# Sums of squares on VectorE, and a low half of weights placed behind the inputs

## The chip, the cores and the metric

One core of one Trainium2 chip. The metric is the device time of one execution in microseconds (us), lower is better. TensorE is called PE, VectorE DVE, ScalarE ACT and GpSimd POOL; SP issues the weight DMAs. L12 is line 12 of the kernel.

## The reference

Two blocks of two layers each work on 256 tokens of width 1024, in float32, one behind the other. Every layer is x = x + mixer(rms_norm(x)), then x = x + mlp(rms_norm(x)); the mixers are a convolution with a gated recurrence (HGRN), stick-breaking attention, a state-space model (S5) with a gated linear unit (GLU), and forgetting attention (fox). The first block modulates its norms and gates with vectors that come from c @ ada_w.

```python
def rms_norm(x, g):
    xf = x.astype(jnp.float32)
    y = xf * lax.rsqrt(jnp.mean(xf * xf, axis=-1, keepdims=True) + EPS)
    return (y * g.astype(jnp.float32)).astype(x.dtype)

def sqrelu_mlp(h, w1, w2):
    a = jnp.square(jax.nn.relu(h @ w1))
    return a @ w2

# one layer of the first block
h = rms_norm(x, norm_mix[layer]) * (1.0 + scale1) + shift1
x = x + gate1 * mixer(h)
h = rms_norm(x, norm_mlp[layer]) * (1.0 + scale2) + shift2
x = x + gate2 * (jnp.square(jax.nn.relu(h @ mlp_w1[layer])) @ mlp_w2[layer])
```

What matters here is the mean of x*x over the 1024 features, of which every norm needs one, and that every product is made to float32's precision.

## The kernel before

The state x lies transposed in SBUF as xT: eight tiles of 128 features by 256 tokens. Every float32 product is made from two halves in the fast format fp32r. ACT copies a weight tile `raw` (128x2048, 1 MB) into its high half `wh`, and DVE makes the low half `wl` = raw - wh; the same is done with the inputs, of which X holds the high halves XH and the low halves XL. A product is wh*XH + wh*XL + wl*XH. Plain 128x128 weights by 256 columns are one matmul.

Weights come as a stream of such tiles, called units, in the order of a plan. `pump` issues a unit's DMA from SP as soon as one of six raw tiles is free; `unit_ahead` makes the halves of up to two units more than the one in use (three pairs of wh and wl tiles), and `release` frees the raw tile once the low half is made. A tuple DMALO names units whose low half would be made by an accumulating DMA; it is empty.

The stages run one after the other: layer 0's mixer (l0), its MLP (mlp0), stick breaking (sb), the second MLP (mlp1), s5 with glu, the third MLP (mlp2), fox, the fourth MLP (mlp3). At the end of each the last products of a stage are finished in eight pieces m = 0 to 7 by three functions: `fin` adds the piece to xT on DVE; `a` makes the next stage's XH of that piece on ACT (`prep_h`) and its square (`square`); `b`, called one piece later, makes XL on DVE (`prep_l`). `square` lets ACT write x*x into one of two tiles sqt, or into sqa for piece 0, and lets POOL add it to sqa. `stats` then multiplies sqa by a matrix of 1/1024 on PE, which adds over the partitions, and ACT turns the result into the scales that the norm needs. At two places (`last=NK - 2`) only five of the seven adds are made, and stats takes the last two squares by themselves. The norm's scale is applied behind the first products, so those start before stats is done.

Order: on POOL and SP it is the program's. On the other engines a list scheduler orders the instructions by priority and by its own costs, except for DVE in s5 with glu and ACT in mlp2 and mlp3, where it is the program's too (ORDER). `behind(later, first, why)` tells the scheduler that one instruction stands behind another on the same engine; no semaphore comes of it. Modulation vectors are made by dot products on DVE (L688, `ada_next`) which are spread over the stages at low priority.

Of the kernel before, what the change touches and what calls it, by code (L numbers as in the profile page):

```python
# [10 lines left out]
F32 = mybir.dt.float32  # L11
F32R = mybir.dt.float32r  # L12
U8 = mybir.dt.uint8
AF = mybir.ActivationFunctionType
# [6 lines left out]
ADD, SUB, MUL, MAX, MIN = ALU.add, ALU.subtract, ALU.mult, ALU.max, ALU.min  # L21

T = 256
D = 1024
NK = D // 128
# [13 lines left out]

DMALO = ()
S5SEQ = "g P0 P1 g T0 T1 TB0 M0 P2 P3 TB1 Q0 Q1 T2 T3 g Q2 Q3"


# [197 lines left out]
class Later:  # L244


    def __init__(self, prog):
        self.ops = []
        for n in ("tt", "ts", "stt", "act", "table", "copy"):
            setattr(self, n, partial(self.do, getattr(prog, n)))  # L250
# [23 lines left out]
class Prog:  # L274
    def __init__(self, ctx, tc, a, out):
        self.ctx, self.tc, self.nc, self.a, self.out = ctx, tc, tc.nc, a, out
        self.vcost = 0.0
        self.bank_last = {}
        self.set_load, self.set_uses = None, []
        self.const = ctx.enter_context(tc.tile_pool(name="const", bufs=1))  # L280
        self.psum = ctx.enter_context(tc.tile_pool(name="ps", bufs=1, space=bass.MemoryType.PSUM))
        self.pball = self.psum.tile([128, 8, 512], F32, name="psall")
        self.pb = [self.pball[:, i, :] for i in range(8)]
# [113 lines left out]
    def unit_ahead(self, ahead, between=None):  # L397

        last = min(self.used_n + ahead, len(self.wseq) - 1)
        while self.split_n <= last:  # L400
            j = self.wseq[self.split_n]
            if j not in self.slot:
                assert self.split_n > self.used_n, ("not loaded", self.plan[j][1])
                break
            b = self.split_n % len(self.hb)
            raw = self.raw_of(j)
            if self.plan[j][1] in DMALO:
                self.act(self.hb[b], raw, AF.Copy)
                self.release(j)
                lo = self.lb[b]  # L410
                self.act(lo, self.hb[b].bitcast(F32), AF.Copy, scale=-1.0)
                self.nc.gpsimd.dma_start(out=lo, in_=self.a["wst"][self.wpos[j]], accum_op=ADD)
                self.split_n += 1
                continue
            n = 1 + (self.plan[j][1][0] in HALVES)
            parts = [slice(i * 2048 // n, (i + 1) * 2048 // n) for i in range(n)]
            for c in parts:
                self.act(self.hb[b][:, c], raw[:, c], AF.Copy)
            if between is not None:
                between()  # L420
                between = None
            for c in parts:
                self.tt(self.lb[b][:, c], raw[:, c], self.hb[b][:, c].bitcast(F32), SUB)
            self.release(j)
            self.split_n += 1
        if between is not None:
            between()
# [76 lines left out]
                wh, wl = (t[:, k, m * 128:(m + 1) * 128] for t in (hv, lv))  # L504
                self.pair(outs[m], wh, wl, self.X2[S][:, k], k == 0, k == NK - 1)

    def rows_mm(self, units, xs, banks, start, stop, evac=None, late=False):

        kt = [(h, l, j) for h, l in units for j in range(2)]
        out = lambda m: self.pb[banks[m // 2]][:, (m % 2) * T:(m % 2 + 1) * T]  # L510
        if evac is not None:
            fin, a, b = evac
        if late:
            for q, m in [(q, m) for q in range(2) for m in range(NK)]:
                h, l, j = kt[q]
                w = h[:, j * D + m * 128:j * D + (m + 1) * 128]
                self.mm(out(m), w, xs[q][0], q == 0 and start and m % 2 == 0, False)
                self.mm(out(m), w, xs[q][1], False, False)
            for q, m in [(q, m) for q in range(2) for m in range(NK)]:
                h, l, j = kt[q]  # L520
                self.mm(out(m), l[:, j * D + m * 128:j * D + (m + 1) * 128], xs[q][0], False, q == 1 and stop and m % 2 == 1)
            return
        for m in range(NK):
            o = out(m)
            for q, (h, l, j) in enumerate(kt):
                c = j * D + m * 128
                xh, xl = xs[q]
                wh, wl = h[:, c:c + 128], l[:, c:c + 128]
                self.mm(o, wh, xh, q == 0 and start and m % 2 == 0, False)
                self.mm(o, wh, xl, False, False)  # L530
                self.mm(o, wl, xh, False, q == len(kt) - 1 and stop and m % 2 == 1)
            if evac is not None and m % 2 == 1:
                for i in (m - 1, m):
                    fin(i, out(i))
                    a(i)
                    if i:
                        b(i - 1)
        if evac is not None:
            b(NK - 1)
# [11 lines left out]
        self.act(self.XH[S][:, m, :T], self.xT[:, m, :], AF.Copy, scale=A[:, m:m + 1])  # L551

    def prep_l(self, S, m, A):
        self.stt(self.XL[S][:, m, :], self.xT[:, m, :], A[:, m:m + 1], self.XH[S][:, m, :T].bitcast(F32), MUL, SUB)

    def prep_shift(self, S, B):
        h = self.XH[S][:, :, 256:257]
# [3 lines left out]
    def square(self, i, last=NK):  # L561

        s = self.sqt[i % 2] if i else self.sqa
        self.act(s, self.xT[:, i, :], AF.Square)
        if 0 < i < last:
            self.nc.gpsimd.tensor_tensor(out=self.sqa, in0=self.sqa, in1=s, op=ADD)  # L566

    def stats(self, bank, std=False, rstd=False, r2=False, epv=False, tok=False, parts=None):
        ps = self.pb[bank]
# [382 lines left out]
    def mlp(self, tag, S, finish, side=(), after=None, before=None):  # L952
        n = DFF // 256
        with self.tc.tile_pool(name="pm" + tag, bufs=1) as p:
            hh = [p.tile([128, 2, T], F32R, name=f"hh{i}") for i in range(3)]
            hl = [p.tile([128, 2, T], F32R, name=f"hl{i}") for i in range(3)]
            tt_ = [p.tile([128, 2, T], F32, name=f"ht{i}") for i in range(2)]
            wb = [p.tile([128, 2], F32, name=f"wb{i}") for i in range(2)]
            yb = (0, 1, 2, 3)

            def A(u):
                b = 4 + 2 * (u % 2)
                t = s = tt_[u % 2]
                ps = [self.pb[b], self.pb[b + 1]]
                self.proj_T((tag + "a", u), S, ps, n=258, parts=1 + (u == 0))
                if u == 0:
                    self.stats(6, std=True, r2=True)
                w = wb[u % 2]
                self.red(w, self.pball[:, b:b + 2, 256:258], ADD)
                for m in range(2):  # L970
                    self.stt(t[:, m, :], self.stdb, w[:, m:m + 1], ps[m][:, :T], MUL, ADD)
                self.act(t, t, AF.Relu)
                self.act(s, t, AF.Square)
                self.act(hh[u % 3], s, AF.Copy)
                self.tt(hl[u % 3], s, hh[u % 3].bitcast(F32), SUB)

            def B(us, fin=None):
                ws = [self.unit((tag + "b", u), ahead=2 - i) for i, u in enumerate(us)]
                xs = [(hh[u % 3][:, j, :], hl[u % 3][:, j, :]) for u in us for j in range(2)]
                self.rows_mm(ws, xs, yb, us[0] == 0, us[-1] == n - 1, fin, (tag + "b", us[0]) in DMALO)  # L980

            def sides(b):
                self.side_banks = (b, b + 1)
                for g, budget in side:
                    start = self.vcost
                    while next(g, "end") == "more" and self.vcost - start < budget:
                        pass

            A(0)
            for u in range(1, n - 1):  # L990
                A(u)
                sides(6 - 2 * (u % 2))
                if u == n - 2:
                    A(n - 1)
                B([u - 1])
                sides(4 + 2 * (u % 2))
            for g, _ in side:
                for _ in g:
                    pass
            if after is not None:  # L1000
                after()
            if before is not None:
                before()
            B([n - 2, n - 1], finish)

    def mlp_finish(self, gate, nxt):
# [824 lines left out]
```

## Time and profile before

| | us |
|---|---|
| median of three runs | 1313.73 |
| lowest and highest | 1310.88, 1315.62 |
| the profiled execution | 1311.48 |
| its span, first to last instruction | 1309.7 |

The profile is of one execution. Busy time is that of an engine's own instructions; a wait is the idle time of an engine before an instruction, put down to what released it last. A name such as `X<-xTt,mod,X` is what an instruction writes and reads; buffer numbers are left out. Consecutive DVE instructions overlap in the rows: one can begin a little before the row of the one before it has ended, so the distance of two starts is less than a row's length.

### The profile page before, as it was taken

What the parts mean: (1) busy time and instruction counts of PE and PEld (TensorE: products, weight loads), DVE (VectorE), ACT (ScalarE), POOL (GpSimd) and SP (SyncE); (2) the same over time, 40 slices, a digit from 0 to 9 for tenths busy, and PEclk for the clock granted to TensorE, in tenths of its full rate; (3) what the DMA queues carried; (4) which work ended last, traced back from release to release, by engine and by line L of the source; (5) the groups of instructions that cost most, each with busy time, mean ns of one, the idle gap of its engine ahead of it and who ended that gap; (6) DMA issues with size and microseconds to landing.
All of it is one profiled execution on the core that took longest, in us unless ns stands there. A gap on an engine that the chain in (4) does not pass through costs nothing.

```text
span 1309.7 us, 22500 instructions
## 1 busy us (share of the span) xinstructions
PE 1225.6 (94%) x9412; PEld 1138.2 (87%) x9412; DVE 1021.1 (78%) x1398; ACT 681.8 (52%) x884; POOL 85.5 (7%) x73
## 2 busy tenths in 40 slices
PE   2999999999999999978889789999999999999997
PEld 2999899999988899978889579887889999888886
DVE  6899999985899969979956857676657786887553
ACT  4545465555548857534555345544545554655442
POOL 0012120000100001000000204000000000100000
PEclk7899999999999999989999899999999999999999
DMA  9867467778365567667579895444555533455520
GB/s 382 325 259 287 201 253 274 279 276 297 131 243 212 205 242 248 249 212 253 180 265 233 233 336 210 160 162 172 214 193 193 193 130 114 156 185 189 213 77 33
DMA packets 63654, 283.84 MB, mean 217 GB/s; under 512 B 8000, under 2 KB 25920, under 8 KB 31936
## 3 DMA queue, kind: packets, MB, share of 16 engines
q1 hardware_dynamic: 63552, 282.40, 60.6%
q8 instruction: 74, 1.21, 0.4%
q14 instruction: 28, 0.23, 0.0%
HBM read 267.70 MB, written 14.68 MB: 216 GB/s over the span
## 4 chain that ended last, share of the span: by engine, by line
PE 68%; DVE 16%; ACT 8%; DMA 4%; issue 3%; POOL 1%; DVEq 0%; ACTq 0%; SPq 0%; POOLq 0%
PE psall L337 67%; DVE wl L314 6%; ACT wh L294 5%; DVE raw L688 2%; DMA raw<-dK 2%; DMA raw<-in_wst_dram 1%; PE psall L340 1%; DMA raw<-dP 1%; DVE tmpn L327 1%; DVE sqt L327 1%; DVE X L327 1%; DVE td L314 1%; POOL sqat L566 1%; DVE sqt L314 0%; ACT X L294 0%
## 5 line engine op out<-in xcount | busy, mean ns | idle before, releaser
L337 PE MATMUL psall<-X,wh 128*128 128x256 f32 (+2 forms) x3360 | 729.3, 308 | 39.7 <-ACT wh L294 23.3
L337 PEld LDWEIGHTS psall<-X,wh 128*128 128x128 f32 x3360 | 544.6, 192 | 78.8 <-ACT wh L294 24.0
L337 PE MATMUL psall<-X,wl 128*128 128x256 f32 (+1 forms) x1992 | 559.2, 284 | 5.9 <-DVE wl L314 5.9
L314 DVE TENSOR_TENSOR wl<-raw,wh 128x2048 fp32r<-128x2048 f32 (+1 forms) x232 | 426.6, 1856 | 108.7 <-ACT wh L294 108.3
L294 ACT ACTIVATE wh<-raw 128x2048 fp32r<-128x2048 f32 (+1 forms) x232 | 354.3, 1546 | 217.3 <-PE psall L337 193.4
L337 PEld LDWEIGHTS psall<-X,wl 128*128 128x128 f32 x1992 | 378.0, 190 | 12.1 <-DVE wl L314 11.3
L337 PE MATMUL psall<-hh,wh 128*128 128x256 f32 x512 | 144.5, 287 | 4.4 <-ACT hh L294 4.3
L337 PE MATMUL psall<-hl,wh 128*128 128x256 f32 x512 | 145.6, 285 | 1.0 <-DVE hl L314 0.9
L337 PE MATMUL psall<-hh,wl 128*128 128x256 f32 x512 | 145.0, 284 | 0.0
L337 PE MATMUL psall<-hid,wh 128*128 128x512 f32 (+1 forms) x432 | 136.3, 372 | 0.0
L566 POOL TENSOR_TENSOR sqat<-sqat,sqt 128x256 f32<-128x256 f32 x52 | 56.2, 1081 | 1054.0 <-ACT sqt L294 1052.9
L337 PE MATMUL psall<-hid,wl 128*128 128x256 f32 x384 | 108.2, 282 | 0.2 <-DVE wl L314 0.2
L337 PEld LDWEIGHTS psall<-hh,wh 128*128 128x128 f32 x512 | 98.0, 193 | 5.6 <-ACT hh L294 5.1
L337 PEld LDWEIGHTS psall<-hl,wh 128*128 128x128 f32 x512 | 98.5, 192 | 1.5 <-DVE hl L314 1.5
L337 PEld LDWEIGHTS psall<-hh,wl 128*128 128x128 f32 x512 | 98.6, 193 | 0.4 <-issue 0.4
L337 PEld LDWEIGHTS psall<-hid,wh 128*128 128x128 f32 x432 | 78.1, 189 | 15.3
L688 DVE CUSTOM_DVE_ANT_0 raw<-raw,adaacc,prmt 128x1024 f32<-128x1024 f32 x64 | 81.4, 1294 | 0.0
L337 PEld LDWEIGHTS psall<-hid,wl 128*128 128x128 f32 x384 | 72.8, 189 | 0.6 <-DVE wl L314 0.6
L294 ACT ACTIVATE tmpn<-psall 128x256 f32<-128x256 f32 (+1 forms) x38 | 17.7, 465 | 62.1 <-PE psall L337 62.1
L314 DVE TENSOR_TENSOR tmpn<-tmpn,psall 128x256 f32<-128x256 f32 (+1 forms) x32 | 17.6, 552 | 38.0 <-ACT tmpn L294 38.0
L688 DVE CUSTOM_DVE_ANT_0 raw<-raw,adaacc,adn 128x1024 f32<-128x1024 f32 x32 | 42.3, 1340 | 4.4 <-ACT td L294 4.4
L294 ACT ACTIVATE ht<-ht 128x512 f32<-128x512 f32 x64 | 40.0, 626 | 6.2 <-DVE ht L327 5.3
(344 smaller groups left out, 1239.6 us busy)
## 6 DMA issues: line engine op xcount, KB each, us to landing
raw<-in_wst_dram SPq DMA_DIRECT2D x231, 1024.0 KB, 4.9
dQ<-s5X SPq DMA_DIRECT2D x8, 512.0 KB, 5.1
dP<-s5X SPq DMA_DIRECT2D x16, 256.0 KB, 3.9
s5X<-in_wst_dram SPq DMA_DIRECT2D x4, 1024.0 KB, 14.8
raw<-dK SPq DMA_DIRECT2D x32, 128.0 KB, 8.4
s5X<-in_s5blk_dram SPq DMA_DIRECT2D x8, 256.0 KB, 3.5
s5X<-dP SPq DMA_DIRECT2D x2, 1024.0 KB, 8.1
raw<-dP SPq DMA_DIRECT2D x2, 1024.0 KB, 12.0
```

Source lines behind the costliest of these rows:

```text
L294: i = self.nc.scalar.activation(out=out, in_=in_, func=func, **kw)
L314: return self.nc.vector.tensor_tensor(out=out, in0=a, in1=b, op=op)
L327: return self.nc.vector.scalar_tensor_tensor(out=out, in0=a, scalar=s, in1=b, op0=op0, op1=op1)
L337: return self.in_bank(out, self.nc.tensor.matmul(out, lhsT=l, rhs=r, start=start, stop=stop))
L340: return self.in_bank(out, self.nc.tensor.transpose(out, in_, self.ident))
L566: self.nc.gpsimd.tensor_tensor(out=self.sqa, in0=self.sqa, in1=s, op=ADD)
L688: self.nc.vector.tensor_tensor_reduce(out=w, in0=w, in1=self.crow, scale=1.0 if sc is None else sc, scalar=b, op0=MUL, op1=ADD, accum_out= ...
```

## The change

`square` lets DVE add instead of POOL. `prep_l` keeps its instruction as `xl_last`, and the first low half of weights that `unit_ahead` issues afterwards is placed behind it on DVE. The branches for DMALO, which no unit takes, go.

```diff
-DMALO = ()
...
-        self.set_load, self.set_uses = None, []
+        self.set_load, self.set_uses, self.xl_last = None, [], None
...
-            if self.plan[j][1] in DMALO:
-                self.act(self.hb[b], raw, AF.Copy)
-                self.release(j)
-                lo = self.lb[b]
-                self.act(lo, self.hb[b].bitcast(F32), AF.Copy, scale=-1.0)
-                self.nc.gpsimd.dma_start(out=lo, in_=self.a["wst"][self.wpos[j]], accum_op=ADD)
-                self.split_n += 1
-                continue
...
             for c in parts:
-                self.tt(self.lb[b][:, c], raw[:, c], self.hb[b][:, c].bitcast(F32), SUB)
+                i = self.tt(self.lb[b][:, c], raw[:, c], self.hb[b][:, c].bitcast(F32), SUB)
+                if self.xl_last is not None:
+                    self.behind(i, self.xl_last, "the inputs first")
+                    self.xl_last = None
...
-    def rows_mm(self, units, xs, banks, start, stop, evac=None, late=False):
+    def rows_mm(self, units, xs, banks, start, stop, evac=None):
...
     def prep_l(self, S, m, A):
-        self.stt(self.XL[S][:, m, :], self.xT[:, m, :], A[:, m:m + 1], self.XH[S][:, m, :T].bitcast(F32), MUL, SUB)
+        self.xl_last = self.stt(self.XL[S][:, m, :], self.xT[:, m, :], A[:, m:m + 1], self.XH[S][:, m, :T].bitcast(F32), MUL, SUB)
...
         if 0 < i < last:
-            self.nc.gpsimd.tensor_tensor(out=self.sqa, in0=self.sqa, in1=s, op=ADD)
+            self.tt(self.sqa, self.sqa, s, ADD)
...
-                self.rows_mm(ws, xs, yb, us[0] == 0, us[-1] == n - 1, fin, (tag + "b", us[0]) in DMALO)
+                self.rows_mm(ws, xs, yb, us[0] == 0, us[-1] == n - 1, fin)
```

`tt` is `tensor_tensor` on DVE; it also adds an estimate of the instruction's time to a running cost, from which the side jobs of mlp0 and mlp1 take their budget.

## Rows read from the trace of the kernel before

**Rows 1.** The page: its span, and the shares of the chain that ended last.

```profile
span 1309.7 us, 22500 instructions
...
PE 68%; DVE 16%; ACT 8%; DMA 4%; issue 3%; POOL 1%; DVEq 0%; ACTq 0%; SPq 0%; POOLq 0%
```

**Rows 2.** Timeline of PE: start, length, work [idle before <- releaser].

```profile
173.30 0.70 PE L337 MATMUL psall<-sqat,onesd 128*128 128x256 f32 x2 [1.83 <-POOL sqat L566]
...
357.70 0.39 PE L337 MATMUL psall<-X,wh 128*128 128x256 f32 x1 [0.59 <-DVE X L327]
...
360.30 0.39 PE L337 MATMUL psall<-X,wl 128*128 128x258 f32 x1 [0.64 <-DVE wl L314]
...
361.75 0.70 PE L337 MATMUL psall<-sqat,onesd 128*128 128x256 f32 x2 [0.83 <-POOL sqat L566]
...
497.20 0.39 PE L337 MATMUL psall<-X,wh 128*128 128x256 f32 x1 [0.91 <-DVE X L327]
...
498.07 0.39 PE L337 MATMUL psall<-X,wh 128*128 128x256 f32 x1 [0.24 <-DVE X L327]
...
796.55 0.39 PE L337 MATMUL psall<-X,wl 128*128 128x256 f32 x1 [0.46 <-DVE wl L314]
```

**Rows 3.** Chain of work, 166 to 174 us: start, length, what.

```profile
170.59 2.66 POOL sqat L566
```

**Rows 4.** Timeline of DVE at the first, second and third boundary.

```profile
169.84 2.83 DVE L314 TENSOR_TENSOR wl<-raw,wh 128x2048 fp32r<-128x2048 f32 x1
...
357.97 2.27 DVE L314 TENSOR_TENSOR wl<-raw,wh 128x2048 fp32r<-128x2048 f32 x1
360.17 1.81 DVE L327 SCALAR_TENSOR_TENSOR X<-xTt,mod,X 128x256 fp32r<-128x256 f32 x2
...
494.00 2.28 DVE L314 TENSOR_TENSOR wl<-raw,wh 128x2048 fp32r<-128x2048 f32 x1
496.20 1.81 DVE L327 SCALAR_TENSOR_TENSOR X<-xTt,mod,X 128x256 fp32r<-128x256 f32 x2
```

**Rows 5.** Instructions by tile: count, ns min/median/max.

```profile
L314 DVE TENSOR_TENSOR xTt<-tmpn,xTt x32: 382/424/494, 347.1 to 1300.8; 128x256 f32<-128x256 f32 x32
L327 DVE SCALAR_TENSOR_TENSOR X<-xTt,prmt,X x32: 475/485/1044, 786.0 to 1122.2; 128x256 fp32r<-128x256 f32 x32
...
L566 POOL TENSOR_TENSOR sqat<-sqat,sqt x52: 726/749/2872, 163.2 to 1279.9; 128x256 f32<-128x256 f32 x52
```

**Rows 6.** Chain of work, 340 to 380 us: one add on DVE.

```profile
351.27 0.34 DVE xTt L314
```

**Rows 7.** DVE by shape, 159 to 176 us: busy us, mean ns.

```profile
L327 DVE SCALAR_TENSOR_TENSOR X<-xTt,mod,X 128x256 fp32r<-128x256 f32 x8 | 4.7, 596 | 0.6 <-ACT X L294 0.6
...
L688 DVE CUSTOM_DVE_ANT_0 raw<-raw,adaacc,prmt 128x1024 f32<-128x1024 f32 x1 | 1.8, 1760 | 0.0
```

**Rows 8.** The same, 345 to 364 us.

```profile
L327 DVE SCALAR_TENSOR_TENSOR X<-xTt,mod,X 128x256 fp32r<-128x256 f32 x8 | 6.5, 820 | 0.0
...
L688 DVE CUSTOM_DVE_ANT_0 raw<-raw,adaacc,prmt 128x1024 f32<-128x1024 f32 x1 | 1.3, 1273 | 0.0
```

**Rows 9.** The same, 485 to 500 us.

```profile
L327 DVE SCALAR_TENSOR_TENSOR X<-xTt,mod,X 128x256 fp32r<-128x256 f32 x8 | 5.0, 639 | 0.2 <-ACT X L294 0.2
...
L688 DVE CUSTOM_DVE_ANT_0 raw<-raw,adaacc,prmt 128x1024 f32<-128x1024 f32 x1 | 1.8, 1757 | 0.0
```

**Rows 10.** Timeline of ACT in the glu loop.

```profile
791.74 0.40 ACT L294 ACTIVATE sqt<-xTt 128x256 f32<-128x256 f32 x1
...
793.68 0.40 ACT L294 ACTIVATE sqt<-xTt 128x256 f32<-128x256 f32 x1
```

**Rows 11.** Chain of work in the glu loop, 785 to 800 us.

```profile
791.87 0.48 DVE X L327
...
794.21 2.30 DVE wl L314
```

**Rows 12.** Timeline of DVE at the fourth boundary.

```profile
726.16 0.42 DVE L314 TENSOR_TENSOR xTt<-tmpn,xTt 128x256 f32<-128x256 f32 x1
```

More of the change, by code (lines that the diff above doesn't have):

```diff
@@ L512, in rows_mm @@
             fin, a, b = evac
[L513 to L522, printed above, removed]
         for m in range(NK):
```

## The prediction

> **What bounds the kernel now.** The page comes first: over half of the chain that ended last is TensorE's [rows 1], so only time in which PE stands can be won. The timeline of PE, taken at the places where one stage hands its sums of squares to the next, shows where it stands. I call these places boundaries and number them in order of time: layer 0 to its MLP at 160 us, MLP to stick breaking at 350, stick breaking to the second MLP at 490, that MLP to s5 at 720, glu to the third MLP at 817, then fox at 1000 and the last MLP at 1120.
>
> At the first, PE stands 1.83 us before the matmul that adds up the sums of squares, released by POOL. At the second it stands three times, for the low half of the inputs (0.59), for a low half of weights (0.64) and for POOL's sum (0.83), 2.06 together. At the third it stands 0.91 and 0.24 for low halves of inputs, 1.15 together. At the boundaries from the fifth on PE stands nowhere, but inside the glu loop it waits 0.46 for a low half of weights [rows 2]. The three stands together are 5.04 us: more the edits can't win there.
>
> Who is late, the chain and the timeline of DVE tell. In the first boundary the chain runs through a POOL add of 2.66 us [rows 3], where the median add takes 0.749 [rows 5]: it began while DVE worked on a low half of weights, and ended with it [rows 4]. In the second and third, the last two low halves of inputs stand right behind a low half of 2.27 and 2.28 us on DVE [rows 4].
>
> **The removed branch.** DMALO is empty, so neither the low half by DMA nor the late matmuls ever ran: 0, whatever covers it. The VectorE helper also adds to a running cost that budgets side work, but only differences inside a side job are used and no square lies there: 0.
>
> **The adds on VectorE.** There are 52: seven at six boundaries, five at the fourth and at the end. No add of these two tiles on DVE is in the trace. The nearest row is the add into xT of the same shape, 0.424 median, 0.382 to 0.494 [rows 5]; in a row of DVE work the next instruction is on after 0.34 [rows 6]. I take 0.34, since the boundaries are such rows: 2.4 us for seven, and 3.0 is the upper end.
>
> What DVE gets back is the slowing by POOL. A low half of inputs takes 0.485 where nothing crosses it [rows 5], but 0.596, 0.820 and 0.639 on average at the three boundaries, eight each: 0.9, 2.7 and 1.2 us. The dot product of the modulation took 1.76 at the first and third against 1.27 at the second: 0.5 more each [rows 7 to 9]. So seven adds cost DVE net 2.4 - 1.4 = 1.0 at the first, 2.4 - 2.7 = -0.3 at the second, 2.4 - 1.7 = 0.7 at the third. That the wide rows are POOL's doing is read from their time alone; below is what it costs if not.
>
> The Trainium skill speaks against the slot of 0.34: its page VectorE: DVE Perf Modes, section The DRAIN you can't avoid, has the next VectorE instruction begin only when the pipe has emptied. The trace disagrees for adds in a row, 0.34 against 0.424; by the rule the sum would be 1.8 us worse, the fourth rival.
>
> **The order.** The first low half of weights after a stage's last low half of inputs now stands behind it on DVE, with no new semaphore. Behind the low half stand only work of the next unit and the release of its raw tile, whose weight DMA then leaves SP's in-order queue a microsecond or two later. Six raw tiles are in flight and PE's list of waits names none for a DMA at a boundary, so I cost that at 0; without that cover the delay itself, at most 2, would be the price. Behind an add stand the low halves of inputs: DVE is in order, and an add waits for ScalarE's square.
>
> First boundary. The low half began at 169.84 and ended at 172.67 [rows 4]. It now has to let pass two low halves of inputs (1.0) and, as I count them, the last three adds (1.0); the four earlier ones (1.4) are paid by the refund (1.4). It takes 2.28 instead of 2.83 and so ends at 169.84 + 2.0 + 2.28 = 174.1, 1.4 later. The wait of 1.83 for the sum goes, and at worst the low half puts 1.4 of it back: a gain between 0.4 and 1.83. I take 1.0, the middle, as the low half had some slack that no row shows.
>
> Second. The low half ended at 360.24. Two low halves of inputs ahead of it (1.0) and a net of -0.3 put its end at 360.9. PE then stands 0.59 + 0.64 + 0.7 = 1.9 there at worst, and no more for the sum, against 2.06: a gain between 0.1 and 2.06, and 1.0 is taken.
>
> Third. The inputs leave 2.28 of low half behind and pay 0.7 for adds, so they come 1.6 earlier. PE waited 1.15 for them: all of it goes. The lower end is 0, if nothing is refunded (2.28 - 2.4). I take 1.15. Together -3.15.
>
> **Where the adds cost.** In s5 and glu DVE's order is the program's, so each add stands between ScalarE's square and the low half of inputs. The chain in the glu loop is tight: input low half at 791.87, weights' low half at 794.21, and PE waits for its end [rows 2, 11]. The first square ends at 792.14 [rows 10]; the add ends its slot at 792.48, so the input's low half comes 0.61 later, and so does the next square, ended at 794.08 before: 794.69. Behind that come add (0.34) and input low half (0.48): the weights' low half starts at 795.5 instead of 794.21, and PE stands 1.3 longer. The lower end is 0, if the engines' new order lifts it; the upper 2.6, if the next turn is late too.
>
> At the fourth boundary the update of xT at 726.16 [rows 12] starts the last square, and stands in a row of DVE work without a gap; up to two adds land ahead of it, 0 to 0.7, and 0.35 is taken. At the fifth to seventh PE rides through without a wait; the cover is its queue of matmuls. Were it gone, 2.4 would show at each boundary that has seven adds.
>
> **Sum.** -3.15 + 1.3 + 0.35 = -1.5. The profiled execution took 1311.48, a span of 1309.7 and 1.78 around it: 1310.0. It lies 2.25 below the median of the runs, 1313.73; from that median the forecast is 1312.2. Its own bounds are -5.04 and -0.5 + 2.6 + 0.7 = +2.8: 1308.7 to 1316.5.
>
> **Rivals.** (a) The three stands go entirely and the glu loop loses nothing, because ScalarE's, PE's and DVE's order is laid anew around the adds: -5.04, 1308.7. For it speaks that the waits are for things that now come by 2 us earlier; against it that glu's DVE order is fixed by hand. (b) Slower: the wide rows on DVE are not POOL's doing, nothing is refunded, and the adds come on top: 1.4 + 2.7 + 1.7 = 5.8 more, +4.3, 1318.0. It decides once less than 0.4 of the 5.8 comes back. Against it: DVE instructions far from POOL's adds keep their narrow time. (c) A wait takes the place of the one removed: PE finds the low half of weights late at the first two boundaries and gains 0.5 there instead of 2.0: 1313.7, no change. (d) Each add holds DVE for its whole 0.424: 21 times 0.084 is 1.8, so +0.3, 1314.0. (e) The order doesn't change, because the low halves stay where they were: without the 1.15 of the third boundary and the 0.59 of the second, +0.2, 1314.0.
>
> **How the numbers follow.** 0.3% is 3.9 us, about what a measurement of this kernel tells from no change. The forecast has a chance of 0.46, (a) 0.22, (b) 0.13, (c) 0.11, (d) 0.04, (e) 0.04. Only (a) is faster by more than 0.3%: 0.22. Only (b) is slower: 0.13. The rest, 0.65, is no change. The range runs from (a), less the 2.85 by which the fastest run before lies under the median, to (b): 1306 to 1318.
>
> **What the profile after would show.** Right: no add on POOL at these places, 52 on DVE of about 0.42; input low halves at the boundaries near 0.48 instead of up to 0.82; the two last of them ahead of a weights' low half at the first three boundaries; PE's stand for POOL gone and 3 us less in all there; in the glu loop a stand of some 1.8 where 0.46 was. Wrong: input low halves still wide; PE waiting over 2 us for a low half of weights at a boundary; or a stand in the long side jobs of the second MLP, whose order the new costs may turn, which no row here can price.

## The result and the profile after

The changed kernel takes 1321.39 us, the median of 7 runs (1318.06 to 1323.34), against 1311.17 of the kernel before on the same chip: a ratio of 1.0063, 95% interval 1.0046 to 1.008. By this ratio it is 8.3 us slower (the two medians lie 10.2 apart), where 1.5 faster was forecast. The profiled execution took 1320.81.

The page of the kernel after, its span and the chain's shares by engine (before: [rows 1]):

```profile
span 1319.0 us, 22471 instructions
...
PE 66%; DVE 19%; ACT 9%; issue 3%; DMA 3%; POOL 0%; DVEq 0%; SPq 0%; ACTq 0%
```

POOL has left the chain and DVE has gained 3 points of it: the work moved as the diff says. Its price, in the view of the tile of sums and then by shape at the second boundary (before: [rows 5, 8]):

```profile
L312 DVE TENSOR_TENSOR sqat<-sqat,sqt x52: 381/420/427, 161.1 to 1289.2; 128x256 f32<-128x256 f32 x52
```

```profile
L325 DVE SCALAR_TENSOR_TENSOR X<-xTt,mod,X 128x256 fp32r<-128x256 f32 x8 | 3.8, 480 | 0.1
```

The add lasts 0.420 and the input's low half is back at 0.480 from 0.820. Both prices are those forecast. The stands of PE are not (timeline of PE, after; the same places as [rows 2], with the second MLP's added):

```profile
172.02 0.39 PE L335 MATMUL psall<-X,wl 128*128 128x258 f32 x1 [0.78 <-DVE wl L312]
...
357.08 0.39 PE L335 MATMUL psall<-X,wh 128*128 128x256 f32 x1 [1.00 <-DVE X L325]
359.62 0.70 PE L335 MATMUL psall<-sqat,onesd 128*128 128x256 f32 x2 [1.55 <-DVE sqat L312]
362.21 0.58 PE L335 MATMUL psall<-X,wl 128*128 128x258 f32 x1 [1.09 <-DVE wl L312]
...
498.54 0.39 PE L335 MATMUL psall<-X,wl 128*128 128x258 f32 x1 [0.47 <-DVE wl L312]
...
580.33 0.79 PE L335 MATMUL psall<-X,wh 128*128 128x258 f32 x2 [12.55 <-ACT s5X L292]
...
803.15 0.50 PE L335 MATMUL psall<-X,wh 128*128 128x256 f32 x2 [0.42 <-DVE tmpn L325]
807.52 0.39 PE L335 MATMUL psall<-X,wl 128*128 128x256 f32 x1 [1.00 <-DVE wl L312]
```

The first boundary fell from 1.83 to 0.78 and the third from 1.15 to 0.47, but the second rose from 2.06 to 3.64, and in the second MLP PE stands 12.55 for ScalarE's copy into s5X (the tile in which the side work of the S5 layer is done). The same place in the kernel before:

```profile
576.41 0.80 PE L337 MATMUL psall<-X,wh 128*128 128x258 f32 x2 [7.38 <-ACT s5X L294]
```

To see what each place cost in all, the clock included, I took from the traces the start of PE's matmuls. Each of these traces has all 9412, in nearly the same order, so the time between, say, the 2440th and the 2680th can be compared. The first row is the kernel before, in us; the other rows are differences from it (e1 to e10 are the experiments below). Columns: the place (b1 to b4: the boundaries; s.br.: stick breaking; "2nd MLP": the stretch of the long stand; "turns": behind it; mlp2: the third MLP), and the matmul that ends the stretch; the first stretch begins with the first matmul.

```
                       start      b1              b2   s.br.      b3         2nd MLP   turns              b4      s5     glu    mlp2    rest
to matmul                880    1200    2440    2680    3500    3800    4200    4320    4700    5360    5600    5960    6200    7200    9400
before                138.98   42.96  148.80   31.79  104.91   37.28   47.01   22.23   50.82   88.47   22.66   39.41   29.75  179.32  311.10
after                  -1.96   -0.80   -0.00   +3.10   -0.25   -1.12   -0.01   +5.17   +0.96   -0.11   +2.14   +2.81   +1.25   -1.67   +0.11
e1 adds only           -0.25   -1.70   -0.01   -1.54   +2.73   -1.70   +1.15   -2.09   +1.08   +0.98   +2.65   -1.53   +1.22   -0.40   +0.01
e2 order only          -1.91   +0.13   -0.00   +2.86   -0.26   -0.32   +0.10   +5.12   +0.58   +1.09   +0.40   +0.26   +0.05   +0.36   +0.83
e3 all lows            -1.55   -0.81   -0.00   +0.11   +1.29   -1.12   -0.01   +5.17   +0.44   +1.04   +2.67   -1.58   +1.22   -1.68   -0.00
e4 adds not b4/glu     +0.72   -0.81   -0.00   +3.16   -0.31   -1.12   -0.01   +5.14   +1.12   -0.03   -0.05   +0.36   +0.05   +0.37   +0.09
e5 not at third        -0.26   -0.86   -0.00   +3.04   -0.25   -1.70   +1.17   -2.75   +2.30   +2.47   +2.13   -0.35   +1.25   -1.70   +0.14
e6 third alone         -2.16   -1.71   -0.01   -1.55   +2.86   -1.12   -0.01   +5.13   +0.61   +2.47   +2.37   -2.83   +1.23   -0.39   +0.02
e7 P on ACT queue      +0.66   -0.81   -0.00   +3.14   -0.29   -1.12   -0.01   -8.35   +2.94   +3.58   +2.67   +0.30   +1.25   -1.69   +0.09
e8 adds not b4         +0.17   -1.73   -0.01   -1.55   +2.75   -1.70   +1.17   -2.34   +2.50   -0.06   -0.04   -0.91   +1.21   -0.39   -0.01
e9 before, P on ACT    -1.64   +0.02   +0.00   +0.00   +1.22   +0.00   -0.01   -8.35   +9.46   -2.49   -0.04   +0.68   +0.05   +0.02   +0.04
e10 e8, P on ACT       -1.49   -1.74   -0.00   -1.55   +4.31   -1.67   +1.16   -7.54   +4.16   -0.91   +0.31   +3.51   +1.24   -0.38   +0.03
```

The first column is no effect of any edit: the engines' order is the same there in all of them, and it moves by 2.9 from one execution to the next. The s5 column, where PE waits for transfers, moves by several us too, and the turns and the stretch behind them move by 1 to 2.6 between kernels with the same edit there. Stick breaking moves by 1.2 in e9, whose program is that of the kernel before up to there (and by 1.6 in e10 against e8). It is the clock of that execution (windows view, before and then e9; columns: stretch, length, busy time of PE, its weight loads, DVE, ACT and POOL, granted clock of PE, DMA share, GB/s):

```profile
368.00:474.00 106.00, 101.50 (x834) 92.06 (x833) 95.82 (x144) 78.39 (x99) 0.00 (x0) 1.00 0.62 239
```

```profile
368.00:474.00 106.00, 101.61 (x824) 92.13 (x823) 95.16 (x141) 77.70 (x99) 0.00 (x0) 0.98 0.62 237
```

The rest repeats to 0.7 between kernels with the same edit at that place. So the loss of the kernel after sits at b2 (+3.10), in the second MLP (+5.17), at b4 (+2.14) and in glu (+1.25); b1, b3 and the third MLP give 3.6 back.

**Second boundary.** The timeline of DVE, after:

```profile
356.54 0.48 DVE L325 SCALAR_TENSOR_TENSOR X<-xTt,mod,X 128x256 fp32r<-128x256 f32 x1
356.94 2.29 DVE L312 TENSOR_TENSOR wl<-raw,wh 128x2048 fp32r<-128x2048 f32 x1
359.14 0.42 DVE L312 TENSOR_TENSOR sqat<-sqat,sqt 128x256 f32<-128x256 f32 x1
359.47 0.48 DVE L325 SCALAR_TENSOR_TENSOR X<-xTt,mod,X 128x256 fp32r<-128x256 f32 x1
359.87 2.29 DVE L312 TENSOR_TENSOR wl<-raw,wh 128x2048 fp32r<-128x2048 f32 x1
```

A low half of weights still stands ahead of the last add and the last low half of inputs. PE's last stand ends at 362.21, with the end of the one at 359.87, so that is the one which PE needs first, the first unit's. The line that holds back clears its own mark after one instruction, so only the first unit's low half was held, and the second's passed it (e3 tests this). The windows view shows the other half of the loss (second boundary, then the fourth):

```profile
359.00:363.00 4.00, 2.30 (x13) 2.11 (x14) 4.00 (x7) 2.29 (x3) 0.00 (x0) 0.87 0.00 0
363.00:367.00 4.00, 4.00 (x27) 4.00 (x26) 2.81 (x3) 1.01 (x4) 0.00 (x0) 0.71 0.92 334
...
736.00:740.00 4.00, 2.87 (x60) 2.90 (x64) 3.97 (x6) 3.24 (x4) 0.00 (x0) 0.67 0.02 4
```

After stands of 3.64 between 356 and 362 PE got 0.71 of its clock, so for part of these 4 us the lower level of 1.2 GHz, and did 27 matmuls; at full clock the same 4 us hold 36 (e3, below). Before, with 2.06 of stands, the clock stayed at 1.00:

```profile
362.00:367.00 5.00, 5.00 (x42) 4.95 (x42) 4.94 (x5) 3.30 (x6) 0.00 (x0) 1.00 0.77 283
```

Of the 3.10, 1.6 are stands and 1.5 the clock. The split is that of this execution: in e4 and e7, which have the same program up to there, the stands are 2.54, the clock lower, and the sum is the same.

**Second MLP.** The chain of waits, after:

```profile
571.96 1.20 DVE raw L671
573.16 0.02 DVE mod L671
...
573.20 0.33 SPq L376
...
573.62 6.04 DMA dP<-s5X
...
579.68 0.61 ACT s5X L292
...
580.33 4.56 PE psall L335 x23
```

Read backwards: PE waits for ScalarE's copy into s5X; the copy waits until the DMA that writes the P maps (dP) has read that tile; the DMA was issued at 573.62, because in SP's queue it stands behind a load of weights (L376), which waits for a raw tile; and the raw tile came free when a dot product of the modulation on DVE (L671) had read it. Before, SP issued the same write at 569.50 (timeline of SP, before):

```profile
569.07 0.33 SPq L378 DMA_DIRECT2D raw<-in_wst_dram  x1
569.50 0.38 SPq L1411 DMA_DIRECT2D dP<-s5X  x1
```

because the freeing dot had run ahead of a low half of weights. After, DVE does the low half first and then the dot (timeline of DVE, before and then after):

```profile
567.75 1.29 DVE L688 CUSTOM_DVE_ANT_0 raw<-raw,adaacc,prmt 128x1024 f32<-128x1024 f32 x1
...
570.89 2.29 DVE L314 TENSOR_TENSOR wl<-raw,wh 128x2048 fp32r<-128x2048 f32 x1 [0.64 <-ACT wh L294]
```

```profile
569.68 2.29 DVE L312 TENSOR_TENSOR wl<-raw,wh 128x2048 fp32r<-128x2048 f32 x1
571.88 1.28 DVE L671 CUSTOM_DVE_ANT_0 raw<-raw,adaacc,prmt 128x1024 f32<-128x1024 f32 x1
```

By the clock of the trace that is 4.1 later; counted from the 4200th matmul (555.64 before, 554.39 after), both the dot and the write come 5.4 later, and the stand is 5.17 longer. And in both kernels the write was late long before that. ScalarE's copy that it reads had ended at 548.25 and 547.01 (timeline of ACT, before and then after), 21.3 and 26.6 before the write left; for most of that time SP stood at a load:

```profile
547.67 0.58 ACT L294 ACTIVATE s5X<-psall 128x512 f32<-128x512 f32 x1
```

```profile
546.43 0.58 ACT L292 ACTIVATE s5X<-psall 128x512 f32<-128x512 f32 x1
```

### The profile page after: what moved, and what is told of

Its sections match the earlier page's. It is cut to its first block, busy times and chain, and to the rows that moved or that the text cites. A ratio compares the mean times of both kernels' runs of the same rounds, so it can differ in the third digit from the quotient of the medians.

```text
span 1319.0 us, 22471 instructions
## 1 busy us (share of the span) xinstructions
PE 1225.7 (93%) x9412; PEld 1138.9 (86%) x9412; DVE 1028.8 (78%) x1450; ACT 681.7 (52%) x884; POOL 28.5 (2%) x21
## 4 chain that ended last, share of the span: by engine, by line
PE 66%; DVE 19%; ACT 9%; issue 3%; DMA 3%; POOL 0%; DVEq 0%; SPq 0%; ACTq 0%
PE psall L335 65%; DVE wl L312 7%; ACT wh L292 5%; DVE raw L671 3%; DMA raw<-dK 2%; DVE tmpn L325 1%; PE psall L338 1%; DVE s5X L312 1%; DVE sqt L325 1%; ACT X L292 1%; DMA raw<-in_wst_dram 1%; DVE td L312 1%; DVE sqat L312 0%; DVE sqt L312 0%; DMA dP<-s5X 0%
## 5 line engine op out<-in xcount | busy, mean ns | idle before, releaser
L671 DVE CUSTOM_DVE_ANT_0 raw<-raw,adaacc,prmt 128x1024 f32<-128x1024 f32 x64 | 80.4, 1279 | 0.0
L671 DVE CUSTOM_DVE_ANT_0 raw<-raw,adaacc,adn 128x1024 f32<-128x1024 f32 x32 | 42.3, 1341 | 4.2 <-DMA raw<-in_wst_dram 4.2
L332 DVE TENSOR_REDUCE wb<-psall 128x2 f32<-128x4 f32 x32 | 5.2, 161 | 39.6 <-PE psall L335 39.3
```

The source lines that it names most:

```text
L332: return self.nc.vector.tensor_reduce(out=out, in_=in_, axis=axis, op=op, **kw)
L671: self.nc.vector.tensor_tensor_reduce(out=w, in0=w, in1=self.crow, scale=1.0 if sc is None else sc, scalar=b, op0=MUL, op1=ADD, accum_out= ...
```

## The experiments

The kernel before gave a median of 1312.42 (17 runs) beside e1 to e4, 1312.91 (26) beside e5 to e8, and 1313.12 (23) beside e9 and e10. Ratios are to it.

**e1: the adds alone.** One theory is that the new order does the harm, its rival that the adds load VectorE and all that follows comes late.

```diff
-                if self.xl_last is not None:
-                    self.behind(i, self.xl_last, "the inputs first")
-                    self.xl_last = None
```

> Adds on VectorE, no order edit. Theory A (three places): the order edit lets the second low half of weights pass the first at the second boundary and moves a dot product of the second MLP behind a low half, so both of these costs go; what stays is the serial DVE chain at the fourth boundary and in the glu loop, together 3 to 5 us over before (PE's stand for s5U and the transposes about 1.5 to 3 us longer, the stand for a low half in the glu loop near 1.0 instead of 0.46). The DVE order in the second MLP is a third one, in which dots come in a burst, so its stand (7.38 before, 12.55 after) is not foretold. Theory B (load): the time of 52 adds on DVE, 17.7 us less a refund of some 6, is the loss, wherever it falls; then this is as slow as the whole change, 8 us over before.

1313.66 us (10 runs), ratio 1.0006, 0.999 to 1.0022: no change, 0.8 us over before where theory A had 3 to 5. The stand in the second MLP, which was not foretold, is 5.30. In the timeline of PE of this run the stands for sums are gone at the first three boundaries; what is left there and behind it is

```profile
357.72 0.39 PE L335 MATMUL psall<-X,wl 128*128 128x258 f32 x1 [0.85 <-DVE wl L312]
...
367.31 0.41 PE L338 MATMUL psall<-cstt,sbvt 128*128 128x128 f32 x2 [1.96 <-issue]
```

The adds win at all three (-1.70, -1.54, -1.70 in the table), and give 2.73 back in stick breaking (6.77 us of stands there for 4.50), 1.15 behind b3, 2.65 at b4 and 1.22 in glu. The theory of the load falls.

**e2: the order alone**, the adds back on POOL.

```diff
-            self.tt(self.sqa, self.sqa, s, ADD)
+            self.nc.gpsimd.tensor_tensor(out=self.sqa, in0=self.sqa, in1=s, op=ADD)
```

> Adds on POOL as before, the order edit alone. Theory A: at the second boundary the low half that is needed second is still made before the last low half of inputs, the one needed first behind it, and PE stands 3 us or more there instead of 2.06; in the second MLP the dot product that frees a raw tile stands behind a low half, as after the whole change, and PE stands 12 to 13 us there instead of 7.38; first and third boundary gain 1 to 2 us each; nothing is lost at the fourth boundary and in the glu loop. Sum: 3 to 6 us over before. Theory B (load of the adds): faster than before by 1 to 3 us.

1321.73 us (4 runs), ratio 1.007, 1.0052 to 1.0088: the whole loss, without the adds. The table puts it at b2 and in the second MLP. It is more than the 3 to 6 us expected: the 1 to 2 us that each of the first and third boundary was to gain did not come (+0.13 and -0.32). Two stands for POOL in the timeline of PE:

```profile
360.71 0.70 PE L335 MATMUL psall<-sqat,onesd 128*128 128x256 f32 x2 [2.95 <-POOL sqat L549]
...
828.67 0.70 PE L335 MATMUL psall<-sqat,onesd 128*128 128x256 f32 x2 [1.35 <-POOL sqat L549]
```

**e3: all low halves of that call behind the inputs**, not only the first.

```diff
                     self.behind(i, self.xl_last, "the inputs first")
-                    self.xl_last = None
             self.release(j)
             self.split_n += 1
+        self.xl_last = None
```

> The whole change, but every low half of weights of that call stands behind the last low half of inputs, not the first alone. Theory A: at the second boundary the two low halves come in the order in which PE needs them; PE's three stands there, 3.64 us after the change, fall to 2 or less; the other places stay, with 12.5 in the second MLP: 1.5 to 3 us less than after the change, 5 to 7 over before. Rival C: the second boundary is slow because two dot products of 1.27 and seven adds stand in it, not because of the swapped low halves; then the stands there change by less than 0.5 us.

1317.74 us (8 runs), ratio 1.0039, 1.0024 to 1.0054. At the second boundary the stands are 2.06 again (timeline of PE), both low halves follow the inputs (timeline of DVE), and the clock stays (windows):

```profile
357.51 0.39 PE L335 MATMUL psall<-X,wh 128*128 128x256 f32 x1 [0.99 <-DVE X L325]
...
361.04 0.39 PE L335 MATMUL psall<-X,wl 128*128 128x258 f32 x1 [1.07 <-DVE wl L312]
```

```profile
358.70 4.49 DVE L312 TENSOR_TENSOR wl<-raw,wh 128x2048 fp32r<-128x2048 f32 x2
```

```profile
363.00:367.00 4.00, 4.00 (x36) 4.00 (x36) 3.40 (x6) 0.29 (x1) 0.00 (x0) 1.00 1.00 406
```

So the low half that passed cost the 3.0 there. The +1.29 in stick breaking is no answer to it: e9 has +1.22 there without any edit, by its clock. The stand of 12.55 is untouched.

**e4: the adds at b4 and in s5 and glu on POOL**, else as after.

```diff
+            if self.on_dve:      # stages l0, mlp0, sb, mlp2, fox, mlp3
                 self.tt(self.sqa, self.sqa, s, ADD)
+            else:
+                self.nc.gpsimd.tensor_tensor(out=self.sqa, in0=self.sqa, in1=s, op=ADD)
```

> The whole change, but the 12 adds at the end of the second MLP (fourth boundary) and in the glu loop stay on POOL. Theory A: the DVE chain there is as before; PE's stands between the last matmul of the second MLP and the first of s5 shrink by 1.5 to 3 us and the stand in the glu loop returns to about 0.5; second boundary and second MLP as after the change: 3 to 4.5 us less than after the change, 4 to 5 over before. Theory B (load): 12 of 52 adds give back 12/52 of 8, 2 us.

1320.12 us (4 runs), ratio 1.0057, 1.0038 to 1.0075: 0.8 less than after, within the noise, where 3 to 4.5 were expected. The 2.14 at b4 and the 1.25 in glu go, but the start of the third MLP then waits for POOL (1.35 at 829.30, the same as in e2), and the column of that MLP goes from -1.67 to +0.37.

**e5 and e6: where the new order does its harm.** In e5 the mark is cleared at the end of stick breaking, so that nothing is held at the third boundary; in e6 at the end of every other stage, so that something is held there alone.

```diff
                 stage()
+                if name not in HELD:    # e5: all but "sb"; e6: only "sb"
+                    self.xl_last = None
```

> The kernel after, but at the third boundary (stick breaking to the second MLP) the low half of weights is not put behind the low halves of the inputs; at the other boundaries it is. VectorE's order in the second MLP is then that of the run with the adds alone. Theory A (the third boundary's rule lays VectorE's side work of the second MLP in another order, and PE pays for it at 568 us): PE's stand there falls from 12.55 to about 5.3, the 3.1 lost at the second boundary stays, the third boundary loses the 0.7 that it had won: 1321.4 - 7.2 + 0.7 = 1315. Theory B (the stand at 568 comes from the adds, or from any of the order edits): the stand stays near 12 and the time at 1321.

> The kernel after, but the low half of weights is put behind the inputs at the third boundary alone. Theory A: the second boundary has no inversion (a stand of 0.85 instead of 3.64, but perhaps 2 us at the transposes after it, as with the adds alone), and the second MLP keeps its stand of 12.5: 1321.4 - 1.5 to 3 = 1318.5 to 1320. Theory B (the cost lies at the first two boundaries): within 1 us of the adds alone, 1313.7, with a stand of 5 to 7 at 568.

e5: 1316.55 us (10 runs), ratio 1.0022, 1.0004 to 1.004. e6: 1321.16 us (5 runs), ratio 1.0049, 1.0032 to 1.0066. The stand in the second MLP, timeline of PE of e5 and then of e6:

```profile
574.88 0.58 PE L335 MATMUL psall<-X,wh 128*128 128x258 f32 x2 [4.85 <-ACT s5X L292]
```

```profile
577.84 0.80 PE L335 MATMUL psall<-X,wh 128*128 128x258 f32 x2 [12.52 <-ACT s5X L292]
```

Theory A holds. One instruction held at the third boundary decides the order in which DVE does its side work in the second MLP: it is that of the adds alone in e5, and that of the kernel after in e6. By differences of ratios, the order at the third boundary costs 0.0063 - 0.0022 = 0.0041 (5.4 us), that at all the others 0.0063 - 0.0049 = 0.0014 (1.8), and the adds 0.0006 (0.8): together 8.0 of the 8.3. By the intervals such a difference is uncertain by some 0.0025 (3.3 us), so only the first is clear of noise; e6 against e1 gives the third boundary 0.0043 (5.6) a second time.

**e7: is the stand SP's queue?** The write of the P maps leaves from ScalarE's queue.

```diff
-                nc.sync.dma_start(out=self.dram["P"][b // 2][:, o:o + 512], ...
+                nc.scalar.dma_start(out=self.dram["P"][b // 2][:, o:o + 512], ...
```

> The kernel after, with one DMA moved: the write of s5's P maps leaves from ScalarE's DMA queue instead of SP's, where it stood behind loads of weights that wait for a raw tile. Theory A (the stand of 12.55 at 568 us is SP's queue: the write is issued late, ScalarE's copy into s5X waits for the tile that the write reads, PE for the copy): the stand falls to 5 or less and the time by 7 or more, to 1314 or below. Rival (ScalarE or the PSUM banks are late by themselves, the DMA only happens to end there): the stand stays over 10 and the time at 1320 or above.

1313.29 us (10 runs), ratio 1.0003, 0.9979 to 1.0026. The stand of 12.55 is gone and nothing of it is left at this place. PE's timeline has its next stands 20 us on:

```profile
588.78 0.43 PE L335 MATMUL psall<-s5X,s5A 128*32 128x128 f32 x8 [2.12 <-ACT s5Kp L292]
...
597.29 1.11 PE L338 MATMUL psall<-cstt,s5A 128*128 128x128 f32 x4 [3.04 <-DVE ht L325]
```

Against the kernel after, the ratio falls by 0.0060, 7.9 us: by the table 13.5 at the stand, of which 2.0 and 3.7 come back in the two stretches behind it. Theory A holds. The write leaves 0.03 after the copy that it reads has ended, where 26.6 lay between (timeline of ACT), and SP's loads stand as long as ever, now with no cost to PE (timeline of SP):

```profile
549.11 0.58 ACT L292 ACTIVATE s5X<-psall 128x512 f32<-128x512 f32 x1
...
549.72 0.35 ACTq L1394 DMA_DIRECT2D dP<-s5X  x1
```

```profile
556.87 21.29 SPq L376 DMA_DIRECT2D raw<-in_wst_dram  x3
```

The writes are also shorter here, 2.5 from issue to landing (median) for 6.0; but 6.0 behind 549.72 would still have ended before the next copy, at 555.83, so the earlier issue was enough for this stand. What the run doesn't separate: the scheduler laid the side work anew with the DMA, from about the 4200th matmul on (six copies into s5X between 546 and 580, where the kernel after has two), so a part of the 7.9 can be the new order's.

**e8: the price of the adds at the fourth boundary.** e1 with the adds on POOL at the end of the second MLP alone.

```diff
+            if self.on_dve:      # every stage but mlp1
                 self.tt(self.sqa, self.sqa, s, ADD)
+            else:
+                self.nc.gpsimd.tensor_tensor(out=self.sqa, in0=self.sqa, in1=s, op=ADD)
```

> The adds alone (no change of the low halves' order), but at the fourth boundary (second MLP to s5) POOL adds as before. Theory A (the adds there stand between the last transposes and updates, which leave no gap on VectorE, and cost PE 2 to 3 us): 1313.7 - 2.5 = 1311.2, with PE's stands after 720 us of 0.6, 0.7, 0.4 and 2.3 as before instead of 1.30, 0.48 and 2.41. Rival (the forecast's 0.35 there is right and the adds alone are level because they win nothing at the first three boundaries): 1313.4, the stands hardly change in sum.

1312.63 us (10 runs), ratio 0.9986, 0.9969 to 1.0002; against e1 that is 0.0020, 2.6 us. The intervals of the two overlap; the table is clearer, with +2.13 to +2.67 at b4 in the six versions with these adds on DVE and -0.05 to +0.40 in the five with them on POOL. Theory A holds, but not as I had put it: the stands there do not grow (5.05 after and 5.14 before between the 5360th and the 5600th matmul, 4.59 in e1 and 5.11 in e8). It is the clock. In e8 the windows view has 1.00 where the kernel after has 0.67 (above) and e1, the second line here, 0.75:

```profile
729.00:733.00 4.00, 2.88 (x71) 2.51 (x72) 3.96 (x6) 3.97 (x6) 0.00 (x0) 1.00 0.02 6
```

```profile
730.00:734.00 4.00, 2.69 (x64) 2.58 (x64) 3.97 (x6) 3.43 (x4) 0.00 (x0) 0.75 0.01 4
```

**e9: the same DMA moved in the kernel before**, with e7's edit and nothing else.

> The kernel before, with one DMA moved and nothing else: the write of s5's P maps leaves from ScalarE's DMA queue. Theory A (the stand in the second MLP is SP's queue in every version, 7.38 before and 12.55 after; the change only moved the instruction that frees the tile): the stand of 7.38 goes as that of 12.55 did; of the 12.55 the time got 7.9 back, so of 7.38 about 4.6: 1312.9 - 4.6 = 1308.3. Rival (the kernel before waits there for something else, and only the order of after made the queue matter): the stand stays near 7 and the time at 1313.

1311.11 us (12 runs), ratio 0.9986, 0.9975 to 0.9997: 1.8 us of the 4.6 expected. The stand of 7.38 is gone (-8.35 in the table), and the 380 matmuls behind it take 9.46 longer. There PE stands 11.93 in all, for 3.84 in the kernel before. The longest of these stands is again for s5X (timeline of PE), and the clock is lower around it (windows):

```profile
602.75 0.80 PE L337 MATMUL psall<-X,wh 128*128 128x258 f32 x2 [4.14 <-ACT s5X L294]
```

```profile
597.00:601.00 4.00, 1.09 (x6) 0.67 (x4) 4.00 (x4) 0.60 (x1) 0.00 (x0) 0.62 0.91 310
601.00:605.00 4.00, 2.25 (x12) 2.02 (x13) 0.88 (x1) 0.87 (x2) 0.00 (x0) 0.50 0.59 183
```

This wait is no longer the queue's. The write that the copy waits for left 0.03 after the copy that it reads, and took 5.57 to land (chain of waits, e9):

```profile
596.45 5.57 DMA dP<-s5X
```

So the mechanism is in the kernel before too, but most of what its stand gives back is spent behind it. Here too the side work was laid anew from about the 4200th matmul on; how much of what comes back is late work that the stand had covered, and how much the new order, is not shown.

**e10: a version to beat both**: e8 with e7's DMA.

> A version meant to beat both: the adds on VectorE except at the fourth boundary, no change of the low halves' order, and the write of s5's P maps on ScalarE's DMA queue. Theory A: what the adds alone win without the fourth boundary (1311.1) and the stand of 5.05 at 568 with the share of 0.63 that came back in the run after with this DMA moved (3.2): 1307.9, that is level with the kernel before with the DMA moved, or 1 better. Rival (the time that the stand frees is given back later in the second MLP, where PE waits for ScalarE's copies instead): 1311.

1310.38 us (12 runs), ratio 0.9975, 0.9958 to 0.9992: faster than the kernel before by 0.25% (3.3 us), the only version that is with adds on DVE. The expectation was 1307.9; the rival, 1311, is nearer: as in e9 much is spent behind the stand (+4.16 behind a gain of 7.54). Its interval overlaps that of e9, so a gain from the adds on top of the moved DMA is not shown.

## Why the prediction was wrong

**The adds: right.** They were 0.420 long, and in a row of DVE work the next instruction was on after 0.33 to 0.34: behind the add at 359.14 the input's low half begins at 359.47. So rival (d) fell: the next instruction does not wait for the end of the one before. The Trainium skill (VectorE: DVE Perf Modes, section The DRAIN you can't avoid), on which that rival leaned, adds itself that a next instruction which is not held starts earlier, and these rows agree. The refund came in full: the inputs' low halves took 0.482, 0.480 and 0.480 at the three boundaries. With the adds alone b1, b2 and b3 gained 4.9 together, nearly the 5.04 of the best rival, but 3.9 of it was lost again in stick breaking and behind b3 (e1).

**The first and third boundary: right.** The stands fell by 1.05 (1.0 forecast) and by 0.68 (1.15); PE passed them 0.80 and 1.12 sooner. But the order won nothing here: the adds alone leave no stand at either (e1), the order puts 0.78 and 0.47 back.

**The second boundary: the first step that failed.** The prediction put two low halves of inputs ahead of "the low half of weights", as if there were one. There are two, and only the first is held. The second passed it, delayed the last add and the last input by 2.29 and then the needed low half by its own place: 3.64 of stands where 1.9 was reckoned at worst. The clock, which stood in no term of the sum, doubled it to +3.10.

**The release of the raw tile: the step that decided.** I put the later release at 0, since six raw tiles were in flight and PE's list named no DMA at a boundary, and named the second MLP's side jobs as what no row could price. The price was 5.4 us (e5). It did not come from the tile released at the boundary: holding one instruction turned the order of DVE's side work, a dot came 5.4 later in the count of matmuls, and SP's queue passed that on to a write that had nothing to do with it (e7). The prediction had expected the costs of the new adds to turn that order; e2 shows that the order edit does it without them. The Trainium skill (Trainium Kernel Development and Optimization, section Key Constraints) says that issuing DMAs from several engines concurrently only saves the sequencer's issue time. In e7 what was saved was time before the issue as well, but 26.6 us of it for that write, not the 0.38 that an issue takes: SP's issuing stood still behind a wait.

**glu: right in size.** 1.3 forecast; the table has +1.25. One stand of 1.8 was foretold; two came, 0.42 and 1.00, for the 0.46.

**The third MLP: not in the sum.** Of the versions with the adds there on DVE, those whose order also holds at the fifth boundary (after, e3, e5, e7) win 1.67 to 1.70, the others (e1, e6, e8, e10) 0.38 to 0.40. No run shows why.

**The fourth boundary: mis-sized.** 0.35 forecast, at most 0.7; +2.14 measured, 2.6 by e8. I had asked how late the last square would be, and had left out of the list of stands that PE stood 5.14 us there already. The adds between the transposes divide PE's stands otherwise, and its clock fell, to 0.67 for the matmuls behind; that the one is why the other happened is argued, not shown.

**The rivals.** (b), the slower one, came nearest in time (1318.0), and that is luck: it needed the refund to fail. One reading was off, without weight in the sum: POOL's add of 2.66 ended at 173.25, 0.58 behind the low half, not with it. Of the signs named, "a stand in the long side jobs of the second MLP" was the one that came.

What stays open: how the scheduler's order follows from the held instruction, and the s5 stretch, which moves by several us between executions (-2.83 to +3.51) without a pattern that these runs explain.

## What to carry to other kernels

An order edge that is meant for one place must be read in the instruction order of the whole stage behind it, and on every instruction of its kind: here the next low half passed the held one, and the side work 70 us later was laid anew. Before costing a late release at nothing, follow its queue: a DMA queue that is issued in order hands the wait for one tile to every transfer behind it, so a write that frees a tile on the critical path should not stand behind loads that wait. And a stand that is removed is worth only what is not late behind it: of 8.35 us in e9, 1.8 reached the end.

## What the runs showed of the hardware

TensorE's granted clock was a term of the sum here. Its two levels are 1.00 and 0.50, 2.4 and 1.2 GHz (e9 has 0.50 throughout 601 to 605 us); values between are means over a stretch with both. Three stands of 1.00, 1.55 and 1.09 within 6 us were followed by a stretch at 0.71, two of 0.99 and 1.07 by one at 1.00; at the fourth boundary nearly the same sum of stands, divided otherwise, gave 0.67 instead of 1.00. The same stands need not give the same clock: through stick breaking the kernel before and e9 run one program, with 4.50 and 4.39 us of stands, and the clock was 1.00 in one and 0.98 in the other, which cost 1.2 us. And the first 880 matmuls of one unchanged piece of program took from 136.8 to 139.7 us in twelve executions, so two profiled executions can differ by 2.9 us before the change begins.
